# HGRN stage of a two-block transformer kernel: its order of work rewritten into 24 slots of two head pairs, with three element-wise steps moved between engines

## Chip, cores and metric

One core of a Trainium2 chip. The metric is device time in microseconds (us) of one execution of the whole kernel. TensorE (PE) multiplies matrices, VectorE (DVE), ScalarE (ACT) and GpSimd (POOL) do element-wise work, SyncE (SP) issues the loads of weights.

## What is computed

The reference runs `first_block` (two layers, 256 tokens, width 1024) and then `second_block`. The change lies wholly in the mixer of the first layer, HGRN2, with 8 heads of 128 keys:

```python
q, z_f, v, g = split(u @ w_in)
q = silu(q)
f = lb + (1 - lb) * sigmoid(z_f)
log_f = log(maximum(f, 1e-30))
k = (1 - lb) * (1 - sigmoid(z_f))
# S_t = diag(f_t) S_{t-1} + k_t v_t^T ;  o_t = S_t^T q_t
o = o * rsqrt(mean(o * o) + eps) * o_gain        # per head
o = o * silu(g)
mix = o @ w_out
h = h + g1 * mix                                  # g1: one of six modulation vectors, c_act @ mod_w + mod_b
```

The same layer needs three more modulation vectors (shift, scale and gate of what follows): vectors 2, 3 and 4 are computed within this stage.

## The kernel before

**Weights.** Every weight matrix is cut into units of 512 KB. `emit_dma` (L185) loads a unit on SP's queue into one of 7 raw buffers. ScalarE casts it to a rounded copy `w_hi` (L192), VectorE takes the difference `w_lo` = raw − `w_hi` (L194), and TensorE multiplies three times (`mm3`, L257 to L259: hi by hi, hi by lo, lo by hi). There are 4 buffers of `w_hi` and of `w_lo`. A raw buffer is free again when VectorE has made `w_lo`, so unit number j can be loaded only when unit j − 7 has been consumed. Units of modulation vectors are used raw: either by TensorE (`total`, L522, as 32-column matmuls of the raw rows) or by VectorE (`gemv_w`, L514 and L516, which accumulate the rows into two tiles `ga` of 128x512, with one `total` against `ones` on TensorE at the end).

**The recurrence.** It is done for pairs of heads (p = 0 to 3) as a tree of levels. `hg_d` (L835) clips f (L838), multiplies it into q (`qp`, L840) and builds a tree of products of f over 2, 4, ... 64 tokens (`dp`, L846). Scores of level l are small matmuls of k by `qp` (`hg_s`: L886 for levels 8 to 3, L905, L899, L892 for levels 2, 1, 0). Between two levels k is multiplied by the tree on POOL and `qp` on VectorE (`hg_u`: L863 and L864, for level 0 L857 and L858). Masked copies (`hg_c`, L916, L920) collect the scores of levels 8 to 3. Then follow the product with v (`pv`), its square (`sq`), the mean (`st`), the root (`r`), the norm and the gate (`hg_n`: L947, L948), the split for the output product (`o`, `ol`: L953, L958).

**The order.** All of it is a hand-written list of tokens, `HG_ORDER` (L49 to L56), and each engine gets its instructions in the order of that list. d, s, u, c, pv, sq, st, r, n, o, ol are the steps above (`s06` is pair 0, level 6). f, v, w, a with two digits or one are one product of weights each: forget gates of pairs 2 and 3, values, output gates g, and the output projection. fa, fb, fc turn the forget product into gates (fc is `gates_of`, L742 to L747); wa, wb, wc make silu(g). y20 to y43 are two units of modulation vector 2, 3 or 4 each, q2 is vector 2's `total`, z2 to z4 finish a vector (`gemv_fin`). Two weight products at most are converted ahead of use.

Of the kernel before, what the change touches and what calls it, by code (L numbers as in the profile page):

```python
# [13 lines left out]
AF = mybir.ActivationFunctionType  # L14
OP = mybir.AluOpType
# [31 lines left out]
tr5 o0 y46 y47 pv4 tr6 o1 o2 z3 q4 pv5 pv6 tr7 o3 pv7 z4 o4 o5  # L47
"""
HG_ORDER = """  # L49
d0 d1 s08 f20 s07 u06 s18 f21 s17 u16 s06 u05 c00 y20 f30 fa2 s16 u15 c10 s05 u04 f31 fb2 s15 u14 s04 u03 c01  # L50
y21 v0 fc2 fa3 s14 u13 c11 s03 u02 d2 v1 fb3 s13 u12 s02 u01 c02 y22 v2 fc3 s12 u11 c12 s01 u00 d3 v3 s11 u10
s00 y23 v4 pv0 sq0 s10 s28 q2 v5 s27 u26 st0 z2 v6 r0 s38 s26 u25 c20 y30 v7 s37 u36 s25 u24 w00 s36 u35 c30 s24
u23 c21 w01 wa0 s35 u34 s23 u22 y31 w10 wb0 pv1 sq1 s34 u33 c31 s22 u21 c22 w11 wc0 wa1 n0 st1 s33 u32 s21 u20
y32 w20 wb1 r1 o0 s32 u31 c32 s20 w21 wc1 n1 pv2 sq2 s31 u30 y33 ol0 w30 o1 wa2 s30 st2 z3 y40 w31 ol1 wb2 r2
pv3 sq3 wc2 wa3 n2 y41 a0 st3 wb3 o2 y42 a1 wc3 r3 ol2 n3 y43 a2 o3 ol3 z4 a3 a4 a5
"""  # L56


# [72 lines left out]
def kernel(ctx: ExitStack, tc: tile.TileContext, x, c, mod_w, mod_b, norm_mix, norm_ffn,  # L131
# [9 lines left out]
    PE, DV, SC, GP, SY = nc.tensor, nc.vector, nc.scalar, nc.gpsimd, nc.sync  # L141
# [24 lines left out]
    def ph(w, name, bufs=2, dt=F32, tag=None):  # L166
        return phase["p"].tile([P, w], dt, name=name, tag=tag or name, bufs=bufs)
# [172 lines left out]
    cols = cst.tile([P, 80], F32, name="cols")  # L340
# [9 lines left out]
    def rows(ap):  # L350
        n = 1
        for d in ap.shape:
            n *= d
        fl = ap
        if len(ap.shape) == 1:
            fl = ap
        elif len(ap.shape) == 2:
            fl = ap.rearrange("a b -> (a b)")
        else:
            fl = ap.rearrange("a b c -> (a b c)")  # L360
        return fl.rearrange("(r p) -> r p", p=P)
# [6 lines left out]
    for n, ap in vb_list:  # L368
        r = rows(ap)
# [4 lines left out]
    def vcol(n):  # L374
        o, r, _ = VB[n]
        return vb_t[:, o:o + r]
# [168 lines left out]
    def gemv_mod(layer, i, gemv=gemv):  # L545
        return gemv(mod_w[layer], D * i, modT[layer][:, 8 * i:8 * i + 8], modb[layer][:, 8 * i:8 * i + 8])
# [88 lines left out]
    st0 = {}  # L635
# [64 lines left out]
    one_lb, lb = cols[:, 8:16], cols[:, 16:24]  # L700
# [24 lines left out]
    T = {}  # L725
# [16 lines left out]
    def gates_of(sg, j):  # L742
        for m in range(2):
            h = 2 * j + m
            s_ = sg[:, 256 * m:256 * m + 256]
            DV.tensor_scalar(T["f"][:, h], s_, one_lb[:, h:h + 1], lb[:, h:h + 1], op0=OP.mult, op1=OP.add)
            DV.tensor_scalar(T["k"][:, h], s_, cols[:, 24 + h:25 + h], one_lb[:, h:h + 1], op0=OP.mult, op1=OP.add)  # L747

    def pair(n, j):
        return T[n][:, 2 * j:2 * j + 2].rearrange("p k t -> p (k t)")  # L750
# [9 lines left out]
    for j in range(2):  # L760
        def ev_f(p, j=j):
            sg = small(512, "sig", 2)
            SC.activation(sg, p, AF.Sigmoid)
            gates_of(sg, j)
        qf_evac.append(ev_f)
    items = {}
    for j in range(2, 4):
        def ev_f2(p, j=j):
            SC.activation(pair("k", j), p, AF.Exp, scale=-1.0)
        for n, st in enumerate(lin_A(wa, 1024 + 256 * j, act("u0"), ev_f2, acc_bank)):  # L770
            items[f"f{j}{n}"] = [st]
        items[f"fa{j}"] = [Step(lambda j=j: sig_a(pair("k", j)))]
        items[f"fb{j}"] = [Step(lambda j=j: sig_b(pair("k", j)))]
        items[f"fc{j}"] = [Step(lambda j=j: gates_of(pair("k", j), j))]
# [60 lines left out]
    def hg_d(p):  # L835

        f = pair("f", p)
        GP.tensor_scalar(f, f, 1e-30, 1.0, op0=OP.max, op1=OP.mult)  # L838
        QP[p] = ph(512, "qp", 4)
        GP.tensor_mul(QP[p], pair("q", p), f)  # L840
        DP[p] = {1: f}
        d, o = ph(504, "dp", 4), 0
        for h in (2, 4, 8, 16, 32, 64):
            two = DP[p][h // 2].rearrange("p (n s) -> p n s", s=2)
            DP[p][h] = d[:, o:o + 512 // h]
            GP.tensor_mul(DP[p][h], two[:, :, 0], two[:, :, 1])  # L846
            o += 512 // h
# [97 lines left out]
    def hg_n(p):  # L945
        o = T["f"][:, 2 * p:2 * p + 2].rearrange("p k t -> p (k t)")
        DV.scalar_tensor_tensor(o, OP_[p], vcol("a_out_norm"), OP_[p, "r"], op0=OP.mult, op1=OP.mult)  # L947
        DV.tensor_mul(o, o, T["sg"][:, 2 * p:2 * p + 2].rearrange("p k t -> p (k t)"))  # L948

    def hg_o(p):  # L950
# [14 lines left out]
    def S_(f, *a, cost=1.0):  # L965
        return Step(lambda: f(*a), [], cost)

    def item(key, f, *a):
        items[key] = [S_(f, *a)]

    LS = ((8, 7), (6, 5), (4, 3))
    for p in range(4):
        for n, f in (("d", hg_d), ("pv", hg_pv), ("sq", hg_sq), ("st", hg_st), ("r", hg_r), ("n", hg_n), ("o", hg_o),
                     ("ol", hg_ol)):
            item(f"{n}{p}", f, p)
        for l in range(9):
            item(f"s{p}{l}", hg_s, p, l)
        for l in range(7):
            item(f"u{p}{l}", hg_u, p, l)
        for n in range(3):  # L980
            item(f"c{p}{n}", hg_c, p, LS[n])
# [6 lines left out]
        items[f"a{n}"] = aproj[n:n + 1]  # L988
    for i in (2, 3, 4):
        g = gemv_mod(0, i, gemv_w if i == 2 else gemv)  # L990
        for n in range(4):
            items[f"y{i}{n}"] = g[2 * n:2 * n + 2]
        if g[8:-1]:
            items[f"q{i}"] = g[8:-1]
        items[f"z{i}"] = g[-1:]
# [254 lines left out]
    items = {}  # L1250
# [11 lines left out]
    for i, g in ((2, g12[NF:]), (3, gemv_mod(1, 3, gemv_w)), (4, gemv_mod(1, 4, gemv_w))):  # L1262
        m = sum(len(s.units) for s in g)
# [557 lines left out]
    items = {"sca": [Step(b2_scale)], "col": [Step(b2_cols)], "cx": [S_(c_x)]}  # L1821
# [4 lines left out]
    for i, it in enumerate(mixers):  # L1826
        kind, p = it
# [49 lines left out]
```

## Time and profile before

| what | value |
|---|---|
| runs | 1177.09, 1178.19, 1177.09 us (median 1177.09) |
| profiled execution | 1175.47 us, span 1173.7 us |
| TensorE busy in the span | 1121.7 us (96%) |
| VectorE, ScalarE, POOL busy | 765.5, 568.4, 153.1 us |
| mean granted TensorE clock | 0.988 |
| the stage of the change | 70.5 to 209.7 us of the span |

The span runs from the first to the last instruction. A group of rows gives for each line of the program the engine, the operation, the tile written and those read, their shape, how many there were, their busy time and the mean of one. The clock is given as a part of full speed: 1.00 is 2.4 GHz and 0.50 is 1.2 GHz.

### The profile page before, as it was taken

Reading aid. Unit: us, or ns where it says so; the run is one execution under the profiler, and the core shown is the slowest. Engines: PE = TensorE matmul, PEld = TensorE weight load, DVE = VectorE, ACT = ScalarE, POOL = GpSimd, SP = SyncE. Lnnn points to the kernel's source line nnn. Section 1 sums busy time; section 2 is a strip of 40 time slices with the busy share of each in tenths; the row PEclk is TensorE's granted clock in tenths of the full one; section 3 lists DMA queues with packets and bytes.
Section 4 is the critical chain, followed back from the end, with each engine's and each line's share of the span. In section 5 each row is a group of like instructions: output and inputs, shape, how many; then the busy total and the mean of one; then the engine's idle time right before and its main releaser. Section 6 shows DMA issues by size and latency. Waiting matters only on the chain.

```text
span 1173.7 us, 23615 instructions
## 1 busy us (share of the span) xinstructions
PE 1121.7 (96%) x9689; PEld 1041.1 (89%) x9689; DVE 765.5 (65%) x1237; ACT 568.4 (48%) x905; POOL 153.1 (13%) x209
## 2 busy tenths in 40 slices
PE   6978889999999999999999999999998999999997
PEld 4867678899999979888999999998898999999997
DVE  2558566677677578885745544667865766766766
ACT  2452445544444555563534434645556544544444
POOL 4046420000000000250000000013322100000000
PEclk9997899999999999999999999999999999999999
DMA  9965657788888768774766566593342656556551
GB/s 265 305 209 162 198 164 277 261 288 290 297 273 289 253 213 269 252 248 149 255 213 197 174 189 185 119 240 122 108 143 75 213 180 210 161 186 198 177 183 54
DMA packets 176124, 241.92 MB, mean 206 GB/s; under 512 B 18712, under 2 KB 142160, under 8 KB 176016
## 3 DMA queue, kind: packets, MB, share of 16 engines
q1 hardware_dynamic: 174928, 239.54, 64.0%
q8 instruction: 76, 1.25, 0.4%
q0 software_dynamic: 912, 0.81, 0.4%
q14 instruction: 32, 0.26, 0.1%
q10 hardware_dynamic: 176, 0.07, 0.0%
HBM read 239.33 MB, written 1.05 MB: 205 GB/s over the span
## 4 chain that ended last, share of the span: by engine, by line
PE 81%; issue 6%; DVE 6%; ACT 3%; POOL 2%; DMA 1%; DVEq 0%; ACTq 0%; POOLq 0%
PE pb_b L257 14%; PE pb_b L259 14%; PE pb_b L258 14%; PE pb_acc L257 10%; PE pb_acc L258 10%; PE pb_acc L259 10%; DVE w_lo L194 2%; ACT w_hi L192 1%; PE pb_b L461 1%; PE pb_gv L522 1%; PE pb_b L1201 1%; DVE nt L571 1%; DVE s L583 1%; DMA vb<-in_a_lb_dram 1%; PE pb_b L1207 0%
## 5 line engine op out<-in xcount | busy, mean ns | idle before, releaser
L194 DVE TENSOR_TENSOR w_lo<-w_raw,w_hi 128x1024 fp32r<-128x1024 f32 (+1 forms) x335 | 409.9, 1248 | 177.0 <-ACT w_hi L192 174.6
L257 PE MATMUL pb_b<-s,w_hi 128*128 128x256 f32 x1488 | 425.4, 286 | 5.1 <-ACT s L1735 2.9
L258 PE MATMUL pb_b<-s,w_hi 128*128 128x256 f32 x1488 | 423.7, 285 | 0.4
L259 PE MATMUL pb_b<-s,w_lo 128*128 128x256 f32 x1488 | 422.6, 284 | 1.4 <-DVE w_lo L194 1.4
L192 ACT CAST w_hi<-w_raw 128x1024 fp32r<-128x1024 f32 (+1 forms) x336 | 341.8, 1043 | 84.2 <-issue 17.0
L257 PEld LDWEIGHTS pb_b<-s,w_hi 128*128 128x128 f32 x1488 | 286.2, 192 | 12.6 <-issue 3.8
L259 PEld LDWEIGHTS pb_b<-s,w_lo 128*128 128x128 f32 x1488 | 286.3, 192 | 2.3 <-DVE w_lo L194 2.2
L258 PEld LDWEIGHTS pb_b<-s,w_hi 128*128 128x128 f32 x1488 | 286.4, 192 | 2.1 <-DVE s L583 0.7
L257 PE MATMUL pb_acc<-s,w_hi 128*128 128x256 f32 x656 | 191.3, 292 | 1.0 <-ACT w_hi L192 1.0
L259 PE MATMUL pb_acc<-s,w_lo 128*128 128x256 f32 x656 | 187.5, 286 | 1.8 <-DVE w_lo L194 1.8
L258 PE MATMUL pb_acc<-s,w_hi 128*128 128x256 f32 x656 | 187.3, 285 | 0.0
L257 PEld LDWEIGHTS pb_acc<-s,w_hi 128*128 128x128 f32 x656 | 127.4, 194 | 5.6 <-issue 3.3
L259 PEld LDWEIGHTS pb_acc<-s,w_lo 128*128 128x128 f32 x656 | 127.3, 194 | 2.4 <-DVE w_lo L194 2.4
L1194 POOL TENSOR_SCALAR att<-att,sm 128x128 f32<-128x128 f32 (+1 forms) x72 | 46.7, 666 | 622.5 <-DVE sm L1187 334.7
L258 PEld LDWEIGHTS pb_acc<-s,w_hi 128*128 128x128 f32 x656 | 127.5, 194 | 0.2
L1048 ACT CAST s<-sig 128x512 fp32r<-128x512 f32 x38 | 23.6, 620 | 120.3 <-DVE sig L1058 120.3
L257 PE MATMUL pb_acc<-w_hi,s 128*128 128x512 f32 x192 | 78.5, 409 | 1.5 <-ACT s L577 1.0
L258 PE MATMUL pb_acc<-w_lo,s 128*128 128x512 f32 x192 | 76.5, 398 | 0.8 <-DVE w_lo L194 0.8
L259 PE MATMUL pb_acc<-w_hi,s 128*128 128x512 f32 x192 | 76.3, 397 | 0.0
L1761 ACT ACTIVATE sig<-att,vb_t,vc_t 128x256 f32<-128x256 f32 x32 | 17.5, 594 | 77.5 <-DVE att L1756 77.5
L1771 POOL TENSOR_TENSOR sig<-sig,rstd 128x512 f32<-128x512 f32 x16 | 22.8, 1428 | 240.2 <-ACT sig L1769 240.2
L1054 ACT ACTIVATE sig<-pb_b 128x512 f32<-128x512 f32 x22 | 13.1, 597 | 81.5 <-PE pb_b L259 81.5
(372 smaller groups left out, 1270.8 us busy)
## 6 DMA issues: line engine op xcount, KB each, us to landing
w_raw<-in_mod_w_dram SPq DMA_DIRECT2D x96, 512.0 KB, 5.2
w_raw<-in_ffn_w_in_dram SPq DMA_DIRECT2D x88, 512.0 KB, 5.4
w_raw<-in_ffn_w_out_dram SPq DMA_DIRECT2D x44, 512.0 KB, 4.9
w_raw<-in_a_w_in_dram SPq DMA_DIRECT2D x32, 512.0 KB, 5.5
w_raw<-in_ffn_w_gate_dram SPq DMA_DIRECT2D x32, 512.0 KB, 3.7
w_raw<-in_ffn_w_up_dram SPq DMA_DIRECT2D x32, 512.0 KB, 5.5
w_raw<-in_ffn_w_down_dram SPq DMA_DIRECT2D x32, 512.0 KB, 3.5
w_raw<-in_kv_mod_w_dram SPq DMA_DIRECT2D x16, 512.0 KB, 5.7
```

What stands on the lines that cost most here:

```text
L192: SC.copy(hi, raw)
L194: DV.tensor_sub(lo, raw, hi.bitcast(F32))
L257: PE.matmul(o, lhsT=whi, rhs=xhi, start=start, stop=False, skip_group_check=True)
L258: PE.matmul(o, lhsT=whi, rhs=xlo, start=False, stop=False, skip_group_check=True)
L259: PE.matmul(o, lhsT=wlo, rhs=xhi, start=False, stop=stop, skip_group_check=True)
L461: PE.matmul(st[:, 0:256], lhsT=mean_d, rhs=sq[:, 256 * m:256 * m + 256], start=j == 0 and m == 0, stop=j == n - 1 and m == 1)
L522: PE.matmul(g[32 * j:32 * j + 32, 0:256], lhsT=by, rhs=r, start=start, stop=stop, tile_position=(0, 32 * j))
L1048: SC.copy(hi, hid)
L1054: SC.activation(sg, g, AF.Silu)
L1194: GP.tensor_scalar(t[:, i, cs], t[:, i, cs], r[:, 2 * b + i:2 * b + i + 1], 1.0, op0=OP.mult, op1=OP.mult)
L1761: SC.activation(zm, am, AF.Identity, bias=vcol("conv_b")[:, f:f + 1], scale=vc_t[:, 64 + f:65 + f])
L1771: GP.tensor_mul(zp, zp, rs_pair())
```

## The change

A new `HG_ORDER` in 24 slots. Each slot has one product of weights (f, v or w; from w30 on the old mix of a and tail tokens), one y unit, and then one level of two pairs side by side: `s06 s16 u06 u16`, first for pairs 0 and 1, then for 2 and 3. Vectors 3 and 4 come first; vector 2, which VectorE accumulates, now comes from y20 just before w21 to y27 before a3, and its total q2 between a3 and a4. Besides: the clip goes from POOL to VectorE; the tree becomes a token `t` of its own, after the products `qp` of both pairs; the gates of pairs 2 and 3 go from VectorE to ScalarE; the norm's last multiply becomes a token `m`; a y token is one unit instead of two.

```diff
 HG_ORDER = """
-d0 d1 s08 f20 s07 u06 s18 f21 s17 u16 s06 u05 c00 y20 f30 fa2 s16 u15 c10 s05 u04 f31 fb2 s15 u14 s04 u03 c01
-y21 v0 fc2 fa3 s14 u13 c11 s03 u02 d2 v1 fb3 s13 u12 s02 u01 c02 y22 v2 fc3 s12 u11 c12 s01 u00 d3 v3 s11 u10
-s00 y23 v4 pv0 sq0 s10 s28 q2 v5 s27 u26 st0 z2 v6 r0 s38 s26 u25 c20 y30 v7 s37 u36 s25 u24 w00 s36 u35 c30 s24
-u23 c21 w01 wa0 s35 u34 s23 u22 y31 w10 wb0 pv1 sq1 s34 u33 c31 s22 u21 c22 w11 wc0 wa1 n0 st1 s33 u32 s21 u20
-y32 w20 wb1 r1 o0 s32 u31 c32 s20 w21 wc1 n1 pv2 sq2 s31 u30 y33 ol0 w30 o1 wa2 s30 st2 z3 y40 w31 ol1 wb2 r2
-pv3 sq3 wc2 wa3 n2 y41 a0 st3 wb3 o2 y42 a1 wc3 r3 ol2 n3 y43 a2 o3 ol3 z4 a3 a4 a5
+d0 d1 t0 t1 y30 f20 f21 s08 s18 s07 s17 c00 c10 u06 u16 y31 f30 fa2 s06 s16 u05 u15 y32 fb2 f31 s05 s15 c01 c11
+u04 u14 fc2 y33 v0 fa3 s04 s14 u03 u13 fb3 y34 v1 s03 s13 c02 c12 u02 u12 fc3 d2 y35 v2 s02 s12 u01 u11 d3 t2 t3
+y36 v3 s01 s11 u00 u10 s28 s27 s38 s37 y37 v4 s00 s10 u26 u36 c20 c30 z3 v5 s26 s36 u25 u35 pv0 sq0 y40 v6 s25
+s35 c21 c31 u24 u34 st0 r0 y41 v7 s24 s34 u23 u33 n0 pv1 sq1 y42 w00 s23 s33 c22 c32 u22 u32 st1 r1 y43 w01 s22
+s32 u21 u31 n1 y44 w10 wa0 s21 s31 u20 u30 wb0 y45 w11 wc0 s20 s30 m0 y46 wa1 w20 o0 wb1 ol0 pv2 sq2 wc1 y47 y20
+w21 m1 st2 r2 pv3 sq3 z4 y21 w30 o1 ol1 wa2 n2 st3 r3 y22 y23 w31 wb2 wc2 m2 n3 y24 a0 wa3 o2 ol2 wb3 y25 a1 wc3
+m3 y26 a2 o3 ol3 y27 a3 q2 a4 z2 a5
 """
...
     def gates_of(sg, j):
         for m in range(2):
             h = 2 * j + m
             s_ = sg[:, 256 * m:256 * m + 256]
+            if j > 1:
+                SC.activation(T["f"][:, h], s_, AF.Identity, bias=lb[:, h:h + 1], scale=one_lb[:, h:h + 1])
+                SC.activation(T["k"][:, h], s_, AF.Identity, bias=one_lb[:, h:h + 1], scale=cols[:, 24 + h:25 + h])
+                continue
...
     def hg_d(p):
 
         f = pair("f", p)
-        GP.tensor_scalar(f, f, 1e-30, 1.0, op0=OP.max, op1=OP.mult)
+        DV.tensor_scalar(f, f, 1e-30, None, op0=OP.max)
         QP[p] = ph(512, "qp", 4)
         GP.tensor_mul(QP[p], pair("q", p), f)
         DP[p] = {1: f}
+
+    def hg_t(p):
+
         d, o = ph(504, "dp", 4), 0
...
         DV.scalar_tensor_tensor(o, OP_[p], vcol("a_out_norm"), OP_[p, "r"], op0=OP.mult, op1=OP.mult)
+
+    def hg_m(p):
+        o = T["f"][:, 2 * p:2 * p + 2].rearrange("p k t -> p (k t)")
         DV.tensor_mul(o, o, T["sg"][:, 2 * p:2 * p + 2].rearrange("p k t -> p (k t)"))
...
-        for n in range(4):
-            items[f"y{i}{n}"] = g[2 * n:2 * n + 2]
+        for n in range(8):
+            items[f"y{i}{n}"] = g[n:n + 1]
```

How the instructions stand on two engines (line numbers of the changed program are higher by one to eleven). **POOL at the start of the stage, before:** clip, product and tree of pair 0, then of pair 1 (`s_256` is f, `s_253` q, `s_255` k), then zero fills and the first key multiply.

```order
L838 TENSOR_SCALAR s_256<-s_256 128x512
L840 TENSOR_TENSOR qp<-s_253,s_256 128x512
L846 TENSOR_TENSOR dp<-s_256 128x256
L846 TENSOR_TENSOR dp<-dp 128x128
L846 TENSOR_TENSOR dp<-dp 128x64
L846 TENSOR_TENSOR dp<-dp 128x32
L846 TENSOR_TENSOR dp<-dp 128x16
L846 TENSOR_TENSOR dp<-dp 128x8
```

The same eight stand there for pair 1, and then the fills (L873, L878) and L863.

**POOL at the same place, now:**

```order
L845 TENSOR_TENSOR qp<-s_253,s_256 128x512 x2
L854 TENSOR_TENSOR dp<-s_256 128x256
L854 TENSOR_TENSOR dp<-dp 128x128
L854 TENSOR_TENSOR dp<-dp 128x64
L854 TENSOR_TENSOR dp<-dp 128x32
L854 TENSOR_TENSOR dp<-dp 128x16
L854 TENSOR_TENSOR dp<-dp 128x8
```

The clips are gone, both products stand first, and the two trees, four fills and two key multiplies (L871) follow.

**VectorE at the end of the stage, now,** from the PSUM copy after w21 (L784) on; L195 is the `w_lo` of a weights unit, L517 an accumulation of vector 2 out of a raw buffer:

```order
L784 COPY s_254<-pb_acc 128x512
L195 TENSOR_TENSOR w_lo<-w_raw,w_hi 128x1024
L959 TENSOR_TENSOR s_256<-s_256,s_254 128x512
L499 TENSOR_TENSOR mod_80<-pb_b,va_t 128x8
L517 SCALAR_TENSOR_TENSOR ga<-w_raw,ca,ga 128x512 x2
L195 TENSOR_TENSOR w_lo<-w_raw,w_hi 128x1024
L969 TENSOR_TENSOR olo<-s_256,ohi 128x512
L758 TENSOR_SCALAR sq<-sq 128x512
L955 SCALAR_TENSOR_TENSOR s_256<-pb_acc,vb_t,rstd 128x512
L517 SCALAR_TENSOR_TENSOR ga<-w_raw,ca,ga 128x512 x4
L195 TENSOR_TENSOR w_lo<-w_raw,w_hi 128x1024
```

Before, no accumulation stood in this part (the first two were just ahead of f30's `w_lo`); now 14 of them and their two first multiplies (L515) alternate with the `w_lo` of the last products.

**VectorE at the same end, before:**

```order
L779 COPY s_254<-pb_acc 128x512
L958 TENSOR_TENSOR olo<-s_256,ohi 128x512
L784 TENSOR_TENSOR s_254<-s_254,sq 128x512
L753 TENSOR_SCALAR sq<-sq 128x512
L947 SCALAR_TENSOR_TENSOR s_256<-pb_acc,vb_t,rstd 128x512
L948 TENSOR_TENSOR s_256<-s_256,s_254 128x512
L194 TENSOR_TENSOR w_lo<-w_raw,w_hi 128x1024 x4
```

Four `w_lo` stood in a row there with nothing between them.

## Rows read from the trace of the kernel before

**Rows 1.** The stage in four windows: start and end, length, then busy time and count of PE, PEld, DVE, ACT, POOL, then the granted TensorE clock, the DMA share and GB/s.

```profile
70.50:95.40 24.90, 15.60 (x287) 14.72 (x290) 14.52 (x22) 8.47 (x10) 16.40 (x23) 0.79 0.42 136
95.40:131.60 36.20, 29.28 (x351) 23.74 (x344) 31.81 (x54) 13.54 (x25) 25.71 (x28) 0.81 0.59 186
131.60:163.00 31.40, 27.91 (x538) 22.87 (x539) 16.11 (x28) 12.04 (x19) 7.99 (x11) 1.00 0.64 199
163.00:209.70 46.70, 46.70 (x467) 40.14 (x469) 29.15 (x46) 26.19 (x43) 4.11 (x6) 1.00 0.67 236
```

**Rows 2.** The stretches of the stage with the lower granted clock, in the same columns.

```profile
74.07:77.48 3.41, 3.23 (x29) 3.17 (x30) 3.41 (x7) 2.46 (x3) 3.33 (x2) 0.50 0.80 300
87.72:94.55 6.83, 5.38 (x54) 5.32 (x55) 4.63 (x9) 0.00 (x0) 3.69 (x7) 0.50 0.18 56
108.20:115.03 6.83, 5.63 (x58) 4.56 (x59) 6.68 (x15) 4.16 (x8) 6.35 (x10) 0.50 0.34 121
121.85:128.68 6.83, 5.43 (x20) 4.59 (x21) 5.43 (x10) 4.44 (x9) 6.36 (x10) 0.50 0.33 106
```

**Rows 3.** First TensorE's waits in the stage, by line: us in total, times, the longest. Then four rows of its timeline: start, us, engine, line, tile, count, and in brackets the idle time before and what ended it; between the last two lie 21 more matmuls.

```profile
PE pb_b L886 <- POOL s L863: 3.5, 1, 3.5
PE pb_b L886 <- DVE s L747: 3.4, 2, 3.1
PE pb_b L886 <- DVE qp L864: 3.1, 1, 3.1
PE pb_b L886 <- POOL qp L840: 2.4, 1, 2.4
PE pb_b L886 <- DVE cb L916: 2.3, 1, 2.3
...
73.69 0.33 PE L886 MATMUL pb_b<-s,s 128*32 128x32 f32 x16 [3.13 <-DVE s L747]
...
79.86 0.28 PE L258 MATMUL pb_acc<-s,w_hi 128*128 128x256 f32 x1
...
82.49 0.28 PE L259 MATMUL pb_acc<-s,w_lo 128*128 128x256 f32 x1
```

**Rows 4.** VectorE at the start of the stage, timeline.

```profile
70.90 1.23 DVE L194 TENSOR_TENSOR w_lo<-w_raw,w_hi 128x1024 fp32r<-128x1024 f32 x1 [0.69 <-ACT w_hi L192]
72.81 0.41 DVE L746 TENSOR_SCALAR s<-sig,cols 128x256 f32<-128x256 f32 x1 [0.68 <-ACT sig L763]
73.14 0.41 DVE L747 TENSOR_SCALAR s<-sig,cols 128x256 f32<-128x256 f32 x1
```

**Rows 5.** VectorE between 90 and 108 us, timeline: accumulations, `w_lo`, a scalar op on 128x512.

```profile
92.05 1.41 DVE L516 SCALAR_TENSOR_TENSOR ga<-w_raw,ca,ga 128x512 f32<-128x512 f32 x2
93.38 2.35 DVE L194 TENSOR_TENSOR w_lo<-w_raw,w_hi 128x1024 fp32r<-128x1024 f32 x2
95.64 0.42 DVE L753 TENSOR_SCALAR s<-s 128x512 f32<-128x512 f32 x1
100.91 2.73 DVE L516 SCALAR_TENSOR_TENSOR ga<-w_raw,ca,ga 128x512 f32<-128x512 f32 x4
```

**Rows 6.** POOL, timeline.

```profile
73.97 2.01 POOL L838 TENSOR_SCALAR s<-s 128x512 f32<-128x512 f32 x1 [54.90 <-DVE s L746]
76.06 2.34 POOL L840 TENSOR_TENSOR qp<-s,s 128x512 f32<-128x512 f32 x1
83.85 1.26 POOL L840 TENSOR_TENSOR qp<-s,s 128x512 f32<-128x512 f32 x1
85.08 0.61 POOL L846 TENSOR_TENSOR dp<-s 128x256 f32<-128x256 f32 x1
85.77 1.94 POOL L846 TENSOR_TENSOR dp<-dp 128x128 f32<-128x128 f32 x5
88.28 0.83 POOL L863 TENSOR_TENSOR s<-s,s 128x256 f32<-128x256 f32 x1
117.05 1.38 POOL L857 TENSOR_TENSOR s<-s,dp 128x128 f32<-128x128 f32 x1
124.74 2.95 POOL L846 TENSOR_TENSOR dp<-dp 128x128 f32<-128x128 f32 x5
```

**Rows 7.** VectorE's groups in the last window, 163 to 209.7 us: line, operation, tiles, count, then busy us and mean ns, then idle time before and its releasers; and one row of all accumulations (min, median, max in ns).

```profile
L194 DVE TENSOR_TENSOR w_lo<-w_raw,w_hi 128x1024 fp32r<-128x1024 f32 x10 | 12.2, 1224 | 5.8 <-ACT w_hi L192 5.7
L784 DVE TENSOR_TENSOR s<-s,sq 128x512 f32<-128x512 f32 x4 | 2.8, 691 | 0.0
L516 DVE SCALAR_TENSOR_TENSOR ga<-w_raw,ca,ga x50: 717/747/1124, 92.0 to 638.6; 128x512 f32<-128x512 f32 x50
```

**Rows 8.** Loads: KB of one and the median us from issue to landing; and what SP's queue waited for between 60 and 210 us.

```profile
w_raw<-in_mod_w_dram SPq DMA_DIRECT2D x96, 512.0 KB, 5.2
pairm<-in_t_pair_dram SPq DMA_DIRECT2D x1, 96.0 KB, 7.5
SPq L185 <- DVE w_lo L194: 43.0, 23, 6.0
SPq L185 <- DVE ga L516: 20.3, 7, 8.2
```

**Rows 9.** ScalarE: the cast of a unit at 67.90, and all Identity operations on 128x256 (min, median, max in ns).

```profile
67.90 1.05 ACT L192 CAST w_hi<-w_raw 128x1024 fp32r<-128x1024 f32 x1
L577 ACT ACTIVATE s<-nt,mod x32: 492/509/513, 19.5 to 561.4; 128x256 fp32r<-128x256 f32 x32
```

More of the change, by code (lines that the diff above doesn't have):

```diff
@@ L972 @@
     for p in range(4):
-        for n, f in (("d", hg_d), ("pv", hg_pv), ("sq", hg_sq), ("st", hg_st), ("r", hg_r), ("n", hg_n), ("o", hg_o),
+        for n, f in (("d", hg_d), ("t", hg_t), ("m", hg_m), ("pv", hg_pv), ("sq", hg_sq), ("st", hg_st), ("r", hg_r), ("n", hg_n), ("o", hg_o),
                      ("ol", hg_ol)):
```

## The prediction
> **What bounds the kernel now.** I read the clock and span first, then the stage by windows, then what TensorE waited for there, then the queues of VectorE and POOL around those waits. The profiled execution took 1175.47 us (span 1173.7); the median of the runs shown is 1177.09, 1.6 us more. The stage that the change rewrites runs from 70.5 to 209.7 us, 139.2 us. In its four windows TensorE is busy 15.60 of 24.90, 29.28 of 36.20, 27.91 of 31.40 and 46.70 of 46.70 us [rows 1]: 19.7 us idle, none of it in the last window. The reader is also to see the granted clock there: 0.79 and 0.81 in the first two windows, 1.00 in the others. It is the lower level (0.50, 1.2 GHz) in four stretches; in these TensorE is busy 3.23 + 5.38 + 5.63 + 5.43 = 19.67 us on work that takes half of that at 2.4 GHz, so 9.8 us go to the clock [rows 2]. Idle time and clock make **29.5 us of loss** in the stage: 13.6 in the first window (9.3 idle, 4.3 clock), 12.4 in the second (6.9 and 5.5), 3.5 in the third, 0 in the last. The other 109.7 us are TensorE work at the full clock, and neither kernel can do without it. So the forecast is a count of what the new order loses.
>
> The waits behind the idle time are named [rows 3]: the first scores for the gates (3.4), scores for POOL's key multiplies and products (3.5, 2.4), scores for VectorE's query multiplies (3.1) and mask copies (2.3). It is a chain: score, multiply on two engines, next score, with one weights product between links.
>
> **What each part costs, engine by engine.** (1) Clip: POOL loses four of 1.92 to 2.01 us [rows 6]; VectorE gains four scalar ops on 128x512, steps of about 0.4 as in its row of 0.42 [rows 5]: nothing on the path, except that pair 0's clip now stands behind a `w_lo`. (2) Gates of pairs 2 and 3: VectorE loses eight of 0.4 [rows 4]; ScalarE gains eight Identity ops of 0.51 [rows 9]. ScalarE is busy 13.54 of 36.20 us where they land [rows 1], so they are covered, but 2 us of them per pair stand ahead of casts (priced in the middle below). (3) Tree split off: the same POOL work, later. (4) One `y` unit per slot: the same 24 loads and 16 TensorE groups, but modulation vector 2, which VectorE computes (16 instructions, two for a unit, as at 92.05 [rows 5]), goes to the end of the stage, and its eight loads on SP's queue with it. (5) The split of the norm's end into `n` and `m`: nothing, the same two instructions. Then the order.
>
> **A, start (70.5 until the scores s16 end).** Before, TensorE stood 3.13 us until 73.69 because s08 needs the gates [rows 3]. Now y30, f20 and f21 go first; both f units were cast before, since the `w_lo` at 70.90 is the last of them [rows 4]. A product of 24 matmuls takes 2.9 us (22 starts in 82.49 − 79.86 = 2.63 [rows 3]), a batch of 16 score matmuls 0.35 [rows 3], a y unit 0.5. The work until s16 is 3 products, 6 score batches and 2 y units: 8.7 + 2.1 + 1.0 = 11.8 us. The other side is POOL. The gates end at about 75.5 (eight steps of 0.33 from 72.81 [rows 4]), one `w_lo` follows, the first clip is done at 77.1. POOL then does two products (2.34 beside `w_lo`, then 1.4 [rows 6]): 80.9. TensorE has been through y30, f20, f21, s08, s18 at 77.6, and waits some 3 us for s07 and s17. Two trees of 2.65 (0.61 and 1.94 plus gaps [rows 6]), four fills (1.3) and two key multiplies (0.84 each) follow: u06 is ready at 88.3, u16 at 89.1. TensorE has finished y31 and f30 at 84.7 and waits 3.6. s16 ends at about 89.5: 19.0 − 11.8 = 7.2 lost, and 1 us for the lower clock: **8**. If POOL is fast all along (products 1.26, nothing low) it is 5.6. If both products take 2.34 and both trees 3.6 (0.61 + 2.95 [rows 6]) it is 11.5. I take 8, as only one `w_lo` is near the first product.
>
> **B, middle (until the last score).** Each link now has two pairs and one product in it: 2.9 + 0.5 + 4 × 0.35 of TensorE work against a VectorE or POOL answer of two key multiplies (about 0.83 each on POOL [rows 6], beside two on VectorE). So most links close without a wait. Two don't. s01 and s11: the two gate groups on ScalarE push the casts of v4 and v5, and their `w_lo` stand ahead of u01 and u11 on VectorE: 0.8. s00: POOL has pair 3's product (1.3), both trees (2.65 each, or 3.6) and u00 (1.38) to do in a line [rows 6], 8.0 to 9.9 us; TensorE has s01, s11, four score batches, y37 and v4, 6.0 us. That is a wait of 2.0 to 3.9, 2.4 taken, since the row of 2.95 stands against one of 1.94. s10 shares a bank of PSUM with s00: 0.5. In all 3.7, **5** with a lower clock of about 1; bounds 2 (only s00, no clock) and 8 (3.9 and two low stretches).
>
> **C, tail (from w21 to a5).** Before, this lost nothing [rows 1]. Now VectorE accumulates vector 2 here. From w21's PSUM copy to the last accumulation it has 36 instructions: 7 `w_lo` in steps of 1.13 (2.35 for two against 1.22), 14 accumulations in steps of 0.66 (2.73 for four), 10 copies and products on 128x512 in steps of 0.6 and five smaller ones [rows 5, 7]: 8.0 + 9.3 + 6.1 + 2.6 = 26.0 us, and 0.7 until the copy begins. q2, the total on TensorE, needs the last of them, and a4 and a5 stand behind q2 in TensorE's queue. TensorE's own work from w21 to q2 is st2 and st3 (0.95 each), pv3 (1.44), z4 (0.2), w30, w31 (2.97 each) and a0 to a3 (11.7): 21.2. So q2 waits at least 5.5. On top come loads: a raw buffer of vector 2 is free only when VectorE has read it, a1's load waits for y21's buffer, a2's for y23, a3's for y24, a5's for y25, and from the issue a load takes 5.2 us [rows 8], the cast 1.05 [rows 9]. If nothing is late this adds 0; if each a unit comes a little late, up to 6; I take 2.3, as most of the wait would be inside q2's. With 2 for the clock (a wait that long was followed by a low stretch before [rows 2, 3]): **10**, bounds 5.5 and 15.
>
> VectorE's rows bear on a rule. Accumulations at 92.05 and 100.91 of 0.747 each took 1.41 for two and 2.73 for four [rows 5, 7]: a step of 0.66, so the next starts before the one ahead has ended. The Trainium skill (VectorE: DVE Perf Modes, Terms, DRAIN) says that the next op can't issue until the pipe is empty. By full durations the 36 instructions would take 28.4 us and C 2.4 more; the trace disagrees and I go by the steps.
>
> **Sum.** 8 + 5 + 10 = 23 us lost, where 29.5 were: −6.5 us. Against the profiled execution's own 1175.47 that is 1169.0; against the median of 1177.09 it is **1170.5**. All lower bounds: 13 lost, −16.5; all upper: 34.5 lost, +5.
>
> **Rivals.** *R1, the tail isn't bound by VectorE.* If waits of VectorE for ScalarE (5.7 us in the old tail [rows 7]) and the new instructions fall together so that the accumulations fill gaps, C costs nothing but its loads: 13 lost, **1160.6**. For it: VectorE is busy 29.15 of 46.70 there now [rows 1], so 17.5 us are free. Against it: they are free early, and y20 can't come sooner than its place. Chance 0.15.
> *R2, the clock falls after each wait.* Waits of 3 us were followed by low stretches of 3.4 to 6.8 us here [rows 2, 3]. With five waits at 2.5 us each in place of 4 the loss is 19 + 12.5 = 31.5: **1179.1**, about no change. For it: the old low stretches all lie in the two windows with most idle time [rows 1, 2]. Against it: TensorE now has 6 us of dense products ahead of its first wait, and the third window with 3.5 us of waits kept 1.00. Chance 0.17.
> *R3, slower by a landing loop in the tail.* Each freed buffer is one load away from the `w_lo` that VectorE needs next, so VectorE, SP's queue and TensorE take turns: release, issue, landing L, cast, `w_lo`, then the next accumulations. SP already waits 43.0 us for `w_lo` reads and 20.3 for accumulations in this stretch of 150 us [rows 8]. Four turns of L + 1.05 + 1.2 make 29.8 us at L = 5.2, which is 8.6 past TensorE's 21.2 and lies within C as forecast; slower than before is the stage when C passes 16.5, that is with turns of 35.7 and L from 6.7 us on. At L = 7.5, as one load of the trace took [rows 8], the turns make 39, the wait 17.8, C 20 and the loss 33: **1180.6**. Against it: L's median is 5.2 over 96 loads [rows 8]. Chance 0.1.
> That the change doesn't do what it says: the instructions of each engine do stand in the new order, and only the waits are open, so a time as before by this cause alone has 0.03.
>
> **Numbers.** Forecast 0.55, R1 0.15, R2 0.17, R3 0.10, rest 0.03. 0.2% (2.35 us) is about what a measurement of this kernel can tell from no change. Faster by over that (under 1174.7): R1, nine tenths of the forecast's case, a little of R2: 0.67. Within it: 0.04 of the forecast's, half of R2 and the rest: 0.14. Slower (over 1179.4): R2's other part, R3: 0.19. The range 1161 to 1182 leaves out half of R1 and part of R3.
>
> **What would show it.** In the new profile: TensorE runs a product at 71 us and waits 3 us before s07 and 3 to 4 before s06, both for POOL; a wait of about 2.4 before s00 for POOL; no wait for a mask copy; then a wait of 5 to 8 us of the `ones` total for the accumulations before a4, with VectorE busy without a gap from w21 to there. The forecast is wrong if that last wait is under 2 (R1), if the stage's clock is under 0.85 with the waits as said (R2), or if VectorE itself waits for ScalarE or loads in the tail (R3).

## Result and profile after

The changed kernel takes **1170.32 us** (median of 4 runs, 1167.38 to 1171.15) against 1177.61 for the kernel before, measured beside it: ratio **0.9933**, 95% interval 0.9914 to 0.9953, which is 5.5 to 10.1 us less. A second measurement gave 1171.24 against 1176.64, ratio 0.9952 (0.9936 to 0.9968), 5.4 us less. The forecast was 1170.5.

The profiled execution of the changed kernel has a span of 1169.2 us, 4.5 less than before's. The stage itself, from its first unit (68.7 us) to the end of a5 (203.0), takes 134.3 us where it took 139.2. The rest of the difference lies outside and has two signs. The changed profile comes to the stage 1.8 us earlier, and behind the stage it loses 2.2 us again. There, between the `kv_w` loads and the second layer's attention, ScalarE waits 7.4 us for those loads, not 4.8, and in 60 us of that stretch TensorE is busy 1.3 us less (56.4 for 57.7); the rest of the 2.2 us is not traced. The same program ran there before and after. In the profiles of the runs below, the stage starts anywhere from 68.7 to 71.9 us; the three latest starts (71.6 to 71.9) are those of e2, e6 and e10, which exchange vectors 2 and 4, and whether the exchange causes this isn't shown. Times of single runs scatter by 2 to 3 us either way (1173.4 to 1179.4 in 22 runs of the kernel before), so I compare the stage's length in the trace as well as the medians.

The stage in four parts (start, middle, the part with no wait, tail), in the columns of [rows 1], and then its three stretches with the lower clock, as in [rows 2]:

```profile
68.70:87.45 18.75, 14.06 (x285) 12.57 (x288) 10.01 (x20) 8.55 (x10) 11.31 (x21) 0.91 0.55 170
87.45:121.50 34.05, 28.58 (x512) 21.39 (x503) 22.73 (x42) 17.91 (x34) 18.49 (x30) 0.94 0.66 218
121.50:166.40 44.90, 44.90 (x599) 36.30 (x598) 24.65 (x44) 20.30 (x38) 8.87 (x12) 0.97 0.54 169
166.40:203.00 36.60, 30.94 (x224) 27.57 (x226) 28.69 (x39) 17.43 (x24) 0.94 (x1) 0.91 0.74 242
...
79.65:83.25 3.60, 3.60 (x23) 3.35 (x17) 0.00 (x0) 0.22 (x1) 2.97 (x10) 0.53 0.62 189
117.20:124.05 6.85, 5.02 (x16) 4.28 (x17) 1.28 (x5) 0.74 (x2) 3.27 (x10) 0.51 0.21 79
192.10:198.85 6.75, 5.48 (x26) 4.20 (x27) 3.10 (x4) 2.26 (x3) 0.00 (x0) 0.52 0.75 259
```

TensorE is idle 4.7, 5.5, 0 and 5.7 us: 15.8 where it was 19.7. At the lower clock it is busy 14.1 us, half of which (7.0) is lost; before, 9.8 were. Counted as in the prediction the loss is 22.9 us, where it was 29.5. That is 6.6 us less, and the stage is only 4.9 shorter: 1.7 us of TensorE's busy time are new. The `y` units make up about that much. A group of 16 matmuls (two units) took 1.07 us, and each of the two groups of eight that replace it takes 0.64; over eight such pairs this makes 1.7 us. First one group of each kernel, then the sum over the stage (four of the 132 belong to the next stage):

```profile
192.98 1.07 PE L522 MATMUL pb_gv<-w_raw,crep 128*32 128x256 f32 x16
133.18 0.64 PE L523 MATMUL pb_gv<-w_raw,crep 128*32 128x256 f32 x8
...
L522 PE MATMUL pb_gv<-w_raw,crep 128*32 128x256 f32 x132 | 9.0, 385 | 0.0
L523 PE MATMUL pb_gv<-w_raw,crep 128*32 128x256 f32 x132 | 10.9, 391 | 0.0
```

No run puts the units back in pairs, so this is read from the trace and not tested.

What TensorE waited for, in the columns of [rows 3]:

```profile
PE pb_b L523 <- DVE ga L517: 3.4, 1, 3.4
PE pb_b L894 <- POOL qp L845: 2.6, 2, 1.8
PE pb_b L900 <- POOL s L865: 2.5, 1, 2.5
PE pb_b L894 <- DVE qp L872: 2.1, 2, 1.6
PE pb_b L907 <- DVE qp L872: 1.7, 1, 1.7
PE pb_acc L260 <- DVE w_lo L195: 1.2, 2, 0.8
PE pb_acc L258 <- DVE s L784: 0.9, 1, 0.9
```

Read from the top: q2 waits for VectorE's accumulations (tail); s07 and s17 for POOL's products (start); s00 for POOL's last key multiply (middle); s06 and s16 for VectorE's multiply (start); s01 for VectorE's multiply (middle); a2 and a3 for `w_lo`; a0 for the PSUM bank that w31's copy releases. Four more lines of 0.3 to 0.5 us are left out. No score waits for a mask copy directly any more, and the first wait for the gates is gone.

POOL at the start, answering to [rows 6] (start, us, ...), and the two rows of VectorE that end the wait of s06 (86.02):

```profile
75.28 3.66 POOL L845 TENSOR_TENSOR qp<-s,s 128x512 f32<-128x512 f32 x2 [57.03 <-DVE s L843]
78.91 0.60 POOL L854 TENSOR_TENSOR dp<-s 128x256 f32<-128x256 f32 x1
79.59 1.66 POOL L854 TENSOR_TENSOR dp<-dp 128x128 f32<-128x128 f32 x5
84.75 1.82 POOL L871 TENSOR_TENSOR s<-s,s 128x256 f32<-128x256 f32 x2
...
84.21 1.25 DVE L924 COPY_PREDICATED cb<-pairm,pb_b 128x128 f32<-128x128 int32 x4 [7.62 <-POOL cb L886]
85.36 1.49 DVE L872 TENSOR_TENSOR qp<-qp,s 128x256 f32<-128x256 f32 x2
```

and in the middle, with VectorE's rows for the same time:

```profile
104.27 1.29 POOL L845 TENSOR_TENSOR qp<-s,s 128x512 f32<-128x512 f32 x1 [2.71 <-DVE s L843]
110.09 1.29 POOL L845 TENSOR_TENSOR qp<-s,s 128x512 f32<-128x512 f32 x1 [3.38 <-DVE s L843]
111.33 1.60 POOL L854 TENSOR_TENSOR dp<-s 128x256 f32<-128x256 f32 x1
113.01 2.78 POOL L854 TENSOR_TENSOR dp<-dp 128x128 f32<-128x128 f32 x5
118.06 0.76 POOL L865 TENSOR_TENSOR s<-s,dp 128x128 f32<-128x128 f32 x2
...
106.58 2.36 DVE L195 TENSOR_TENSOR w_lo<-w_raw,w_hi 128x1024 fp32r<-128x1024 f32 x2 [2.46 <-ACT w_hi L193]
109.53 0.42 DVE L843 TENSOR_SCALAR s<-s 128x512 f32<-128x512 f32 x1
```

Here is a step that the prediction did not have (its item 1 priced the clip at nothing here): POOL stands idle 3.38 us before pair 3's product, because the clip that it needs is now on VectorE, behind two `w_lo`, which wait for casts behind the gates on ScalarE. s00 (118.52) pays for it: from the product to u00's multiply POOL's line takes 8.35 us (110.09 to 118.44), and without the idle time it would end at 115.1, when TensorE comes to s00 at 115.97 (an estimate from these rows).

VectorE in the tail, the first and the last of its rows:

```profile
167.02 0.69 DVE L784 COPY s<-pb_acc 128x512 f32<-128x512 f32 x1 [2.55 <-ACT sq L783]
167.96 1.23 DVE L195 TENSOR_TENSOR w_lo<-w_raw,w_hi 128x1024 fp32r<-128x1024 f32 x1 [0.24 <-ACT w_hi L193]
173.83 2.73 DVE L517 SCALAR_TENSOR_TENSOR ga<-w_raw,ca,ga 128x512 f32<-128x512 f32 x4
185.90 2.36 DVE L195 TENSOR_TENSOR w_lo<-w_raw,w_hi 128x1024 fp32r<-128x1024 f32 x2 [0.48 <-ACT w_hi L193]
192.56 1.41 DVE L517 SCALAR_TENSOR_TENSOR ga<-w_raw,ca,ga 128x512 f32<-128x512 f32 x2
```

From 167.02 to 193.97 is 26.95 us, with 0.7 us of gaps for ScalarE at the two places shown. The forecast was 26.0 of work. The four accumulations take 2.73 as before [rows 5]: steps of 0.66 where one takes 0.743 (median), so each starts before the one ahead has ended.

### The profile page after: what moved, and what is told of

The parts are those of the page before. It is cut to its first block, busy times and chain, and to the rows that moved or that the text cites. A ratio compares the mean times of both kernels' runs of the same rounds, so it can differ in the third digit from the quotient of the medians.

```text
span 1169.2 us, 23616 instructions
## 1 busy us (share of the span) xinstructions
PE 1121.8 (96%) x9689; PEld 1037.5 (89%) x9689; DVE 759.7 (65%) x1233; ACT 572.0 (49%) x913; POOL 138.3 (12%) x205
## 3 DMA queue, kind: packets, MB, share of 16 engines
HBM read 239.33 MB, written 1.05 MB: 206 GB/s over the span
## 4 chain that ended last, share of the span: by engine, by line
PE 78%; DVE 7%; ACT 5%; DMA 4%; issue 3%; POOL 2%; SPq 0%; DVEq 0%; ACTq 0%; POOLq 0%
PE pb_b L258 14%; PE pb_b L260 14%; PE pb_b L259 14%; PE pb_acc L258 10%; PE pb_acc L260 9%; PE pb_acc L259 9%; DVE w_lo L195 2%; ACT w_hi L193 2%; PE pb_b L462 1%; DMA w_raw<-in_a_w_in_dram 1%; DMA w_raw<-in_kv_w_dram 1%; POOL dp L854 1%; DVE ga L517 1%; PE pb_b L1212 1%; PE pb_gv L523 1%
## 5 line engine op out<-in xcount | busy, mean ns | idle before, releaser
L195 DVE TENSOR_TENSOR w_lo<-w_raw,w_hi 128x1024 fp32r<-128x1024 f32 (+1 forms) x335 | 409.4, 1245 | 180.9 <-ACT w_hi L193 173.4
L193 ACT CAST w_hi<-w_raw 128x1024 fp32r<-128x1024 f32 (+1 forms) x336 | 341.4, 1042 | 82.6 <-DMA w_raw<-in_a_w_in_dram 18.8
```

The costliest lines, as they stand in the source:

```text
L193: SC.copy(hi, raw)
L195: DV.tensor_sub(lo, raw, hi.bitcast(F32))
```

## Experiments

Theory T: each stall that is left is the queue of one engine (POOL at the start and in the middle, VectorE in the tail). "Stage" is the length in the profile from the end of the products ahead of it to the end of a5: 139.1 before, 134.3 and 133.7 in two profiles of the changed kernel. Each ratio is to the kernel before, measured beside the run, with its 95% interval. Of the variants of the changed kernel only e10 has an interval clear of both of the changed kernel's own (0.9914 to 0.9953 and 0.9936 to 0.9968); the others are read by where their waits moved and by the stage.

**e1, tree of pair 2 ahead of pair 3's clip.** `- d3 t2 t3` / `+ t2 d3 t3`.

> The changed kernel with one token moved: the tree of pair 2 (t2) goes ahead of pair 3's clip and product. Theory T (each of the three remaining stalls is a queue of one engine; here POOL's line product 3, two trees, last key multiply): in the changed kernel POOL stands idle from 106.7 to 110.1 us while it waits for pair 3's clip, and the tree of pair 2 then takes 4.46 us. It fits into that idle time, so u00 is done 2.4 to 4.5 us sooner: the wait of 2.55 us before s00 and the 0.51 before s10 go, and with them the low clock from 116.9 to 123.9 us (about 2.5 us). T expects 4 to 5.5 us less than the changed kernel, about 1165.5. Rival C (the clock finds another place to fall, or the same multiply waits for VectorE instead): 1 to 2 us less, about 1169. Rival N (those waits were no part of the sum): no change, 1170.3.

1167.77 us, ratio 0.9932 (0.9918 to 0.9946); stage 132.0, 2.4 shorter, of which 1.2 lies in the middle. The wait before s00 (2.55) is gone, but half of that was taken back on the spot:

```profile
108.97 1.61 POOL L854 TENSOR_TENSOR dp<-s 128x256 f32<-128x256 f32 x1
110.66 3.56 POOL L854 TENSOR_TENSOR dp<-dp 128x128 f32<-128x128 f32 x5
...
108.89 2.78 DVE L195 TENSOR_TENSOR w_lo<-w_raw,w_hi 128x1024 fp32r<-128x1024 f32 x2 [2.46 <-ACT w_hi L193]
111.59 1.05 DVE L872 TENSOR_TENSOR qp<-qp,dp 128x256 f32<-128x256 f32 x2
```

The tree (5.25 us, 2.3 at the start) and VectorE's two `w_lo` (2.78, alone 2.36) slow each other, the multiplies before s01 come later, and s01 waits 2.3 where it waited 1.7 (the profile names POOL's tree as what ended it). The clock found other places too: it is at the lower level from 88.5 to 92 us, behind the waits of s06 and s16, and from 112 to 116, behind s01's, and no longer in f30 and at s00. So both forms of rival C came in part; T's size was twice too large.

**e2, vectors 2 and 4 exchanged.** `y4n` and `y2n` change names; `- z4 ... a3 q2 a4 z2 a5` / `+ q2 z2 ... a3 a4 z4 a5`.

> The changed kernel with the units of modulation vectors 2 and 4 exchanged: VectorE's accumulations stand in slots 9 to 16 (y40 to y47's places), q2 and z2 follow them, and TensorE's vector 4 stands in the tail. Theory T (VectorE's queue of 27 us bounds the tail): the wait of 3.35 us before q2, the low clock from 192 to 198.7 us (2.7 us) and most of the 2.3 us of waits of a0 to a3 go, 6 to 8 us less in the tail; VectorE is busy 20.5 of 31.4 us in slots 9 to 16 and gets 11 us more there, which may cost up to 4. About 1166, between 1162.5 and 1170.5. Rival R1 (the tail waits for loads and casts, VectorE is not the bound): the a units wait as before and the time stays at 1169 to 1171. Rival R3 (landing loop): as R1, but with VectorE idle in the tail.

1167.26 us, ratio 0.9919 (0.9903 to 0.9935); stage 128.3, 6.0 shorter, as T had it. The time is only 3 to 4 us under the changed kernel's: this profile comes to the stage 3.3 us later. No a unit and no q2 waits in the tail; slots 9 to 16 have no wait at all with VectorE's accumulations in them. R1 falls with it, with one limit: TensorE itself now frees the raw buffers in the tail, so loads come earlier here as well. That loads weren't the bound is seen in the changed kernel's own tail, where no cast of ScalarE waits for a load and VectorE waits 0.7 us for casts. One new wait of 2.8 us stands in the tail, for ScalarE's copy of vector 2's total right behind q2, and a low clock after it.

**e3, clip back on POOL.** `- DV.tensor_scalar(f, f, 1e-30, None, op0=OP.max)` / `+ GP.tensor_scalar(f, f, 1e-30, 1.0, op0=OP.max, op1=OP.mult)`.

> The changed kernel with the clip of f back on POOL, nothing else. Theory T (POOL's chain sets the start): two clips of about 1.95 us return to POOL ahead of the products, so s07 waits about 2 us more, and u06 and u16 come some 4 us later, of which s06 and s16 feel 2 to 4; in the middle pair 3's clip no longer stands behind two w_lo on VectorE, so product 3 starts about 1.4 us sooner and s00 waits 1.4 less. Net 1.5 to 3.5 us more than the changed kernel: about 1172.8. Rival P (the clip's engine does not matter, the gain comes from the order alone): 1170.3, within 1 us.

1172.80 us, ratio 0.9966 (0.9954 to 0.9977); stage 135.6, 1.3 longer. The start is 1.8 us longer (20.6), as T said. In the middle s01 waits 0.7 (not 1.7), but another 1.6 is lost one score earlier and s00 still waits 2.4, so the part gained nothing. The sum is right, its second term was not: POOL's own clip took 2.81 us there, where the idle time for VectorE's had been 3.38.

**e4, gates of pairs 2 and 3 back on VectorE.** `- if j > 1:` / `+ if j > 9:`.

> The changed kernel with the gates of pairs 2 and 3 back on VectorE, nothing else. Theory T: the four Identity operations of 2.36 us leave ScalarE twice, so the casts of v4 and v5 start sooner, and eight scalar operations of 0.41 return to VectorE where it had a gap of 2.46 us: the two cancel, s01 waits between 0.5 and 2 us, the time is within 1.2 us of 1170.3. Rival G (ScalarE's gates are what holds s01 and through the casts s00): 2 to 3 us less, 1167.8. Rival H (VectorE has no room for them): 2 to 3 us more, 1172.8.

1171.18 us, ratio 0.9961 (0.9948 to 0.9973); stage 134.3. s01 waits 2.2, s00 2.1: the two cancel as T said. This part of the change is worth nothing that these runs can tell.

**e5, trees of pairs 2 and 3 behind u00 and u10.** `- d3 t2 t3` ... `u00 u10` / `+ d3` ... `u00 u10 t2 t3`.

> The changed kernel with the trees of pairs 2 and 3 (t2 t3) put behind the last multiplies of pairs 0 and 1 (u00 u10). Theory T: POOL's line ahead of u00 shrinks from product, two trees and multiply to product and multiply, so the wait of 2.55 us before s00 goes (0.5 before s10 stays), and the low clock from 117 to 124 us with it; the trees then run beside v4, s00, s10 and v5, and u25 needs them only after s26. The stage, 134.3 us in the changed kernel's profile, becomes 129.5 to 131.5; the time about 4 us under the changed kernel. Rival V (contention: when trees run beside VectorE's w_lo and multiplies both slow down, as with t2 early, where t2 took 5.25 us and the multiplies before s01 came 0.6 later): the wait moves to s26 or u25 and the stage stays above 133.

1170.10 us, ratio 0.9953 (0.9940 to 0.9967); stage 133.4. The wait before s00 is gone, and this one stands in its place:

```profile
PE pb_b L497 <- DVE cb L924: 2.7, 1, 2.7
```

z3 needs a PSUM bank that the masked copies c20 and c30 release; they need the zero fills of pairs 2 and 3, and the fills now stand behind both trees on POOL. T was right on the queue and wrong on the size, since I had moved the trees past u00 but ahead of the fills. V named the size, not the reason.

**e6, e5 and e2 together.** `z4` moved behind a5.

> The changed kernel with both: vectors 2 and 4 exchanged as before, trees late, and z4 behind a5 (there it waited 2.8 us for ScalarE's copy). Theory T (the stalls are independent queues, so the gains add): stage 134.3 less 6 for the exchange, less 3 to 4.5 for the trees, less 2.8 to 4 for z4 (the wait and the low clock behind it): 121.5 to 124 us, 110 of it work; the time 10 to 12 us under the changed kernel, about 1159. Rival A (VectorE is full in slots 9 to 16 once the trees run beside its accumulations): the gains of trees and exchange overlap, stage about 128, time about 1164.

1166.74 us, ratio 0.9920 (0.9906 to 0.9934); stage 130.3. T missed by 7 us. The wait behind q2 was z2's, not z4's; so my edit had moved the wrong token, and it was 3.9 us here, besides 2.5 at z3 as in e5. A's number is nearer, but VectorE was not full: TensorE waits for no accumulation in this profile.

**e7, kernel before with f20 and f21 ahead of the first scores.** `- s08 f20 s07 u06 s18 f21 s17 u16` / `+ f20 f21 s08 s18 s07 u06 s17 u16`.

> The kernel before with one piece of its order changed: f20 and f21 go ahead of the first scores (f20 f21 s08 s18 s07 u06 s17 u16). Theory T (POOL's line clip, product, tree, clip, product, tree sets the start, TensorE only waits elsewhere): the wait of 3.13 us for the gates goes and comes back before s07, s17 and s06; the time until s16's end and the total are within 1.5 us of the kernel before. Rival O (the order of the products makes the gain at the start): about 3 us less than before, and the low clock at 74 us gone as well, 4 to 5 in all.

1175.47 us, ratio 1.0000 (0.9988 to 1.0012). O falls, T holds. The wait for the gates went and came back behind POOL:

```profile
PE pb_b L886 <- POOL qp L840: 7.6, 2, 6.2
```

**e8, old order with clip and trees moved.** The changed code with the old list, `d0 d1 t0 t1` at its head, gates on VectorE.

> The kernel before in its old order with two element-wise moves of the change alone: clip on VectorE, and at the start both products qp ahead of both trees (gates all on VectorE, vector 2 early as before). Theory T: POOL's line until u06 loses 3.9 us of clips, and s17 and s06 come 2 to 4 us sooner; later d2 and d3 lose 1.9 us each on POOL, of which s02 and s00 feel some. The total is 3 to 6 us under the kernel before. Rival O (the order alone gives the gain): within 1.5 us of before. Rival S (the clip behind w_lo on VectorE costs what POOL gains): 1 to 3 us slower.

1175.95 us, ratio 0.9998 (0.9986 to 1.0011), stage 139.5: no change, where T wanted 3 to 6 and O none. The start did get shorter as T said (22.2 us until s16's end, 24.8 before), and at s10's end the run is still 2.7 ahead. It loses them behind that, not by a longer wait, but by the clock, which fell twice where it had stayed at 2.4 GHz before [rows 2]:

```profile
128.45:131.60 3.15, 3.15 (x8) 2.48 (x9) 1.23 (x1) 1.25 (x2) 0.00 (x0) 0.50 0.66 219
148.60:152.15 3.55, 3.55 (x32) 3.51 (x19) 0.94 (x3) 0.00 (x0) 0.82 (x1) 0.54 0.34 126
```

Half of 6.7 us is 3.3. The first followed a wait of 3.24 before s10, which the order before does not have; the second followed the wait of 2.30 before s24, which it has as well, with the clock staying up. (e7 has that wait too, and a granted clock of 0.57 over the 4 us from 150.)

**after_again, the changed kernel on the chip of the last two.**

> The changed kernel once more, on the chip of the runs that follow, so that they can be compared with it directly. Its waits (1.8 and 0.8 at s07 and s17, 1.6 at s06, 1.7 at s01, 2.6 at s00, 3.4 at q2) are set by the queues and come back to within 0.2 us each; what differs between its runs lies ahead of the stage and in the second layer's loads. Theory T: ratio to the kernel before 0.992 to 0.996. Rival J (most of the gain was a lucky set of load landings, since the profile's stage is only 4.8 us shorter): 0.996 or more.

1171.24 us, ratio 0.9952 (0.9936 to 0.9968); stage 133.7. All waits came back to within 0.3 us (s00 2.8; T had 0.2). The ratio is as T had it, and J's 0.996 lies just inside the interval.

**e9, POOL's line put in the order of need.** `- d3 t2 t3 ... u00 u10 s28 s27 s38 s37 ... s00 s10 u26 u36 c20 c30` / `+ d3 ... u00 u10 s28 s27 s38 s37 u26 u36 t2 t3 ... s00 s10 c20 c30`.

> The changed kernel with POOL's line in the middle put in the order in which TensorE needs it: u00 u10, then the fills of pairs 2 and 3 and u26 u36, then the trees t2 t3 (in the run with the trees late the fills and u26 stood behind the trees, and the wait moved to the masked copies that z3 waits for). Theory T (POOL's line is the bound in the middle): no wait at s00 and none over 1 us at z3; the trees end at about 120 us, when s26 is read; the stage, 134.3 us, becomes 129 to 131, the time 3 to 5 us under the changed kernel of the same call. Rival V (trees beside VectorE's w_lo and multiplies cost as much wherever they stand): the wait turns up at u25 or s25 and the stage stays above 133.

1165.97 us, ratio 0.9923 (0.9900 to 0.9947); stage 128.4, 5.3 shorter than in the profile of after_again; 0.9 of that lies in the tail, where the order is the same. No wait at s00, none at z3, and the clock stays at 1.00 from s16 to q2. The middle, to set beside the second row of the changed kernel's windows:

```profile
88.55:118.90 30.35, 27.27 (x515) 20.51 (x504) 23.79 (x42) 17.89 (x33) 16.19 (x21) 1.00 0.73 230
```

V falls: it is the order on POOL's queue, not contention, that cost the most. POOL still stands idle 3.37 us before pair 3's product, and s00 doesn't wait: so the late clip holds s00 only together with the two trees.

**e10, e9 and the exchange, z2 behind n2 and z4 behind a5.**

> The last one and the exchange of vectors 2 and 4 together, with z2 put some tokens after q2 (behind q2 it waited 2.8 us for ScalarE's copy of the total, and a low clock followed) and z4 after a5. Theory T: the stage goes from 134.3 to 121 to 125 us, 110 of it work; the time 9 to 13 us under the changed kernel of the same call. Rival A (VectorE full in slots 9 to 16): stage 128, time 6 under it.

**1156.51 us**, ratio **0.9837** (0.9816 to 0.9858), 14.7 under the changed kernel measured beside it, more than T's 9 to 13; stage 121.1, as T had it. All of TensorE's waits in the stage that are left:

```profile
PE pb_b L894 <- DVE qp L872: 3.6, 2, 3.0
PE pb_b L894 <- POOL qp L845: 2.6, 2, 1.8
PE pb_b L907 <- DVE qp L872: 1.6, 1, 1.6
PE pb_b L900 <- DVE cb L924: 0.9, 1, 0.9
PE pb_b L913 <- DVE qp L872: 0.3, 1, 0.3
PE pb_acc L260 <- issue: 0.2, 1, 0.2
...
71.70:90.65 18.95, 12.76 (x285) 11.30 (x288) 10.15 (x20) 8.60 (x10) 11.34 (x21) 0.99 0.55 167
90.65:122.35 31.70, 28.62 (x512) 21.49 (x503) 23.63 (x42) 17.90 (x34) 16.08 (x21) 0.95 0.69 219
122.35:161.15 38.80, 38.78 (x542) 34.07 (x540) 32.86 (x56) 19.94 (x36) 12.07 (x21) 1.00 0.59 184
161.15:192.85 31.70, 31.59 (x276) 26.84 (x276) 20.83 (x27) 18.05 (x26) 0.95 (x1) 1.00 0.89 308
```

From s10 to a5 TensorE is idle 0.1 us and VectorE works 53.7 of 70.5 us: the accumulations fit once they stand where VectorE is free. What is left is mostly the start, as long as ever (6.2 us idle; 3.1 in the middle, with a low stretch of 4 us at 90).

## Why the prediction was right, step by step

**The count of losses held, its terms less so.** Forecast 8 + 5 + 10 = 23 us lost; by the same count 6.5 + 8.0 + 8.4 = 22.9. That the three errors cancel to 0.1 us is luck. So is a median 0.2 us from the forecast: the forecast took the stage to be as much shorter as the loss is smaller (6.5 us), the stage is 4.9 shorter (5.4 in the second profile), since one `y` unit per slot, priced at nothing, costs TensorE 1.7 us by the trace; and the medians differ by 7.3 and by 5.4 us in the two measurements.

- *A, start:* 18.75 us against 19.0 forecast; lost 6.5, forecast 8. POOL's line ran as said: products done 10.2 us into the stage (forecast 10.4), key multiplies of pair 0 at 16.9 (17.8), since a tree took 2.3, not 2.65. Two waits for POOL came at s07 and s17 (2.6, forecast 3). The one at s06 was 1.6, not 3.6, and ended with VectorE's multiply, which stands behind the mask copies, which wait for POOL's fills. f30, partly at the lower clock, took 4.5 us of TensorE's time. In e1 and e10 it ran at 2.4 GHz in 3.1 us and s06 waited 3.0, with the start as long (18.8 and 18.95): here the clock cost nothing, POOL decided. e3 adds two clips to its line and the start grows by 1.8. So POOL's part is shown. (The bounds of A, worked out again from the prediction's own terms, are about 6 and 11, not 5.6 and 11.5.)
- *B, middle:* 8.0 lost, 5 forecast, at the edge of its bound. s00 waited 2.55 (2.4 forecast). From 110.09 on POOL's line took 8.35 us (8.0 to 9.9 forecast), one tree in it 4.46 beside `w_lo`, and TensorE 5.9 (6.0). What the prediction lacked is that this line began late, after 3.38 us in which POOL waited for the clip; s01, which waits for the same two `w_lo`, held TensorE back as well, and so the difference came out as forecast. The mis-sized terms are s01, 1.9 with s02 for 0.8, and the clock, 2.5 for 1; 0.5 before a matmul of v4 was in no term. e9 shows that POOL's order is the cause of s00's wait: it leaves only s01's 1.6, 0.3 at s02 and 0.9 at s10 there.
- *C, tail:* 8.4 lost, 10 forecast. The queue of VectorE was sized within 1 us, and q2 waited for it; I had allowed 8 us of waits, there were 5.7 (3.4 at q2, 2.3 at a0, a2 and a3) and 2.7 of clock for 2. TensorE's own work until q2 was 21.3 (21.2 forecast). So the 5.5 that two queues leave held, and the 2.3 added for late loads did not come: the waits of the a units came out of q2's, which is therefore 3.4 and not the 5 to 8 that the prediction wanted to see there. e2 shows the cause: without the accumulations there the waits are gone.
- *Clock:* 4 forecast over all, 7.0 measured; waits 19 forecast, 15.8 measured. These two errors cancel as well.

**The rivals.** R1 falls: VectorE's queue was full for 27 us and q2 waited 3.4 us at its end, where R1 wanted under 2 (e2 agrees). R3 falls: VectorE waited 0.7 us for casts in the tail, so no turn of load, cast and accumulation decided. R2 falls by its own sign: the clock is 0.91 to 0.97 in the four parts, not under 0.85. It fell three times and not five, each time in a wait or behind one, and took 7 us by the count; its mechanism is seen in e8, where it ate the gain.

**What gains.** Neither piece gives anything in the old order in the end: not the products ahead of the scores (e7, 1.0000), nor clip and trees (e8, 0.9998, a gain of 2.7 us lost again to the clock). The two were not run together in the old order. With two pairs side by side, the clip's move is worth 1.3 us of stage in one profile (e3) and the gates' move nothing (e4). So most of the gain seems to lie in the new list itself: slots of two pairs with one product between the links, which give a score a product's time to be answered, and the order within them. This follows by exclusion and isn't shown; the slots were not run apart from the order of the vectors, which alone costs 6 us of stage (e2).

## What to carry to other kernels

When an order is written by hand, list each engine's queue in the order of need and look at what stands ahead of the one instruction that the bound engine waits for: here two trees ahead of a 0.4 us multiply cost 4 to 5 us of stage (e9), and accumulations put at the end 6 (e2). A wait removed at a dependence comes back at the next one if the queue behind it is as long (e5, e7); fix the queue. Work without a deadline belongs where its engine is idle, not at the end where everything has one.

## What the runs showed of the hardware

- The same wait of 2.30 us before s24 was followed by a low clock in e7 (0.57 over 4 us) and e8 (0.54 over 3.55 us) and not in the kernel before (1.00): so one wait does not decide it, and a change that moves waits about can lose through the clock what it gains in time.
- POOL's tree of six products takes 2.3 us while VectorE is quiet (78.91 on) and longer beside VectorE's `w_lo` and multiplies: 3.3 in e9, 3.5 in e5, 4.5 in the changed kernel, 5.3 in e1. VectorE's slow down too (in e1 two `w_lo` 2.78 for 2.36; two query multiplies 1.05 for 0.75).
- A low clock during a product cost nothing where the next score had to wait for POOL anyway: the start is 18.75 us with the clock at 0.91, and 18.77 (e1) and 18.95 (e10) with it at 1.00 and 0.99.
